# Places for loaded weights, the split of y, and how the last heads' rows are turned, in a two-layer decoder trunk

## The chip, the cores and the metric

The kernel runs on one core of one Trainium2 chip. The metric is the device time of one execution in microseconds (us). The core has five engines with queues of their own: TensorE (PE; its weight loads are listed as PEld), VectorE (DVE), ScalarE (ACT), GpSimd (POOL) and SyncE (SP). Here SP's queue issues every DMA, in order. An engine that waits at an instruction runs nothing that is queued behind it.

## The reference

Two pre-norm residual layers and a final norm, over 1024 positions of width 1024, all in float32:

```python
x = x + lru_mixer(rms_norm(x, g0), ...)   # layer 0: conv, gates, linear recurrence, width 1536
x = x + fox_mixer(rms_norm(x, g1), ...)   # layer 1: attention, 16 heads of 64
return rms_norm(x, final_g)

def fox_mixer(h, w_in, b_f, w_out):
    u = h @ w_in                            # q, k, v, gate: 1024 each; 16 forget logits
    cum = cumsum(log_sigmoid(f_logit + b_f))
    logits = (q @ k.T) / 8 + (cum[query] - cum[key])      # causal
    o = softmax(logits) @ v
    return (o * silu(gate)) @ w_out
```

## The kernel before

Every large product is done in three passes: a float32 operand is split into a high part in float32r (`to_hi`) and a low rest (`to_lo`), and TensorE adds high·high, low·high and high·low. So weights, values, probabilities and the gated outputs y all pass through a pair of splitting instructions: `to_hi` mostly on ACT, `to_lo` on DVE or POOL.

**Loaded weights.** A DMA brings weights into a place of the tag `wf` of the pool `wpool`, and the split writes them to places of `wh` and `wl` (four of each). A place is free again once its last reader is done. `wf` has three places. The largest user sets a place's size: the first values' weights, two blocks of 256 values and 16 forget logits, 2304 bytes in each partition; all others need 2048 or less. `wf` is used for layer 0's weights (`weights`, `out_weights`, `split_gates`), for q, k and gate weights and most of the output weights (`weights`), for the values of heads 4 to 15 (`value_weights`, in three groups of four heads) and for the last two pairs' output weights (`late`).

**Attention.** `values(0)` makes the values of heads 0 to 3 and the forget logits; `forget` turns the logits into cumulative sums. Then head after head, each in two passes, written out by hand as strings: `"1.0.1.10.1..0"` for a head's first pass, `"10.1.0.10.1.0.0"` for its second (`LAST` has longer ones for heads 12 to 15, with more dots). In the first pass 0 is a step of `weigh(hd, 0)` (queries 0 to 511 times values) and 1 a step of `maxima(hd, 1)` (scores, maximum and exponential of query rows 7, 6, 5, 4, a row being 128 queries). In the second pass 0 is `weigh(hd, 1)` and 1 is `maxima(hd + 1, 0)` (rows 3 to 0). A dot is a piece of `fill`, some six matmuls of the projections of the next pair of heads (for heads 12 to 15: of the output projection, `partial` and `turned`), and one step of `side`.

Each row's scores S lie in one of two places of PSUM (tag `S`); DVE masks and finds the maximum (L773), ACT makes the exponential p (L778).

**Turning p.** Values are multiplied with p turned, keys on partitions. `by_dma(hd, c)` says which way: by TensorE (`transpose`, L61, into a PSUM place of tag `S`, then split from there by ACT and DVE), or for part of the blocks "far": for the last two of a half's four rows, DVE turns 32 by 32 blocks (L733), a DMA writes them to DRAM (`turnd`, L738 and L740), and four DMAs read them back (`pp<-turnd`, L745), whereupon ACT and DVE split them. Before, only head 0's first half is turned by TensorE alone.

**y.** `side` of a second pass is `settle(hd)`: it fetches the reciprocals of the sums (`recb`), has POOL scale the gate with them (L813) and, for an odd head, multiply the pair's first half of y by it (`gated`, L911), and then `put_away(hd, 0)`: ACT splits y (`yh`), DVE makes the rest in place (`yo`), two DMAs store both to DRAM (`y1d`, L928). The second half's `put_away(hd, 1)` stands in `put_later`, the side of the next head's first pass, at its fourth dot. This holds for pairs 0 to 5; `load_y` fetches them back during head 13. `yo` has two places, so that a pair's first half of y takes the place of the pair before's.

**Order.** The program is written in this order, but a planner reorders each engine's queue by its own estimate of when operands are ready; `issue_after` ties an instruction behind another one of its engine (`seen`: the last exponential on ACT; `masked`: the last maximum on DVE).

**Memory.** Layer 1's pools `tu` and `at` lie where layer 0's `x`, `y`, output weights and squares lay; in `at` the tags lie in the order of their first use, in before: `yo`, `recb`, `sg`, `ph`, `p4`, `p5`, `pp1`, `turn`, and so on.

Of the kernel before, what the change touches and what calls it, by code (L numbers as in the profile page):

```python
# [17 lines left out]
P = 128  # L18
SEQ = 1024
HALF = 512  # L20
KT = 8
# [17 lines left out]
def trunk(ctx: ExitStack, tc: tile.TileContext, xt, w0, wg, wo0, pc, gn, gf, w1, wv, wf, bf, wo1, out):  # L39
# [60 lines left out]
    def split_weights(src, shape, hi_eng, lo_eng, parts=wpool):  # L100
        n = shape[0] * shape[1]
        room = -(-n // 64) * 64
        a = wpool.tile([P, room], F32, tag="wf", name="wf", bufs=3)[:, :n]
        b = parts.tile([P, room], F32R, tag="wh", name="wh")[:, :n]
        c = parts.tile([P, room], F32R, tag="wl", name="wl")[:, :n]
        wt, hi, lo = (t.rearrange("p (a b) -> p a b", a=shape[0]) for t in (a, b, c))
        for part, sl in src:
            nc.sync.dma_start(wt[:, :, sl], part)
        to_hi(b, a, hi_eng)
        to_lo(c, a, b, lo_eng)  # L110
        return [(hi[:, k], lo[:, k]) for k in range(shape[0])]
# [67 lines left out]
    with ExitStack() as l0:  # L179
# [85 lines left out]
        gate_weights = {}  # L265

        def split_gates(n):
            wt = wpool.tile([P, 4, P], F32, tag="wf", name="wgf", bufs=3)[:, :2]
            nc.sync.dma_start(wt, wg[n])
            wgh = tmp.tile([P, 2, P], F32R, tag="wgh", name="wgh", bufs=2)  # L270
            wgl = tmp.tile([P, 2, P], F32R, tag="wgl", name="wgl", bufs=2)
            to_hi(wgh, wt, nc.vector)
            to_lo(wgl, wt, wgh, nc.vector)
            gate_weights[n] = wgh, wgl
# [80 lines left out]

        def out_weights(g, d0, parts=wpool):

            wt = wpool.tile([P, 4, P], F32, tag="wf", name="wf", bufs=3)
            for j in range(2):
                nc.sync.dma_start(wt[:, 2 * j : 2 * j + 2], wo0[d0 + j, :, 2 * g : 2 * g + 2])  # L360
            hi = parts.tile([P, 4, P], F32R, tag="wh", name="wh")
            lo = parts.tile([P, 4, P], F32R, tag="wl", name="wl")
            to_hi(hi, wt, nc.scalar)
            to_lo(lo, wt, hi, nc.vector)
            return [[(hi[:, 2 * j + i], lo[:, 2 * j + i]) for i in range(2)] for j in range(2)]
# [136 lines left out]
    with ExitStack() as l1:  # L502
# [24 lines left out]
        def value_weights(g, parts):  # L527

            waiting = []
            for k in range(0, KT + 2, 2):  # L530
                if k < KT:
                    wt = wpool.tile([P, 2, 256], F32, tag="wf", name="wf", bufs=3)
                    nc.sync.dma_start(wt, wv[g, :, k : k + 2])
                    waiting.append(wt)
                if k:
                    own = wpool if k <= 4 else vwpool
                    hi = own.tile([P, 2, 256], F32R, tag="wh", name="wh")
                    lo = own.tile([P, 2, 256], F32R, tag="wl", name="wl")
                    with tc.issue_after(seen[0].ins):
                        to_hi(hi, waiting[0], nc.scalar)  # L540
                    with tc.issue_after(masked[0].ins):
                        to_lo(lo, waiting.pop(0), hi, nc.vector)
                    parts += [(hi[:, i], lo[:, i]) for i in range(2)]
                yield

        def values(g, parts):

            ex = 0 if g else HEADS
            for k in range(0, 0 if g else KT, 2):
                src = [(wv[g, :, k : k + 2], slice(0, 256)), (wf[:, k : k + 2], slice(256, 256 + ex))]  # L550
                parts += split_weights(src, (2, 256 + ex), nc.scalar, nc.gpsimd)
                if k == 2:
                    yield
            Vs[2 * g], Vs[2 * g + 1] = [], []
            for st in range(8):
                if ex and st % 2:
                    pt = ps.tile([P, SEQ], F32, tag="S", name="vps")[:, : 256 + ex]
                else:
                    pt = ps.tile([P, 256 + ex], F32, tag="g", name="vps")
                c = (st % 4) * P  # L560
                for k in range(KT):
                    xh, xl = hT[st // 4][k]
                    wh, wl = parts[k]
                    xh, xl = xh[:, c : c + P], xl[:, c : c + P]
                    matmul(pt, xh, wh, start=k == 0, stop=False)
                    matmul(pt, xl, wh, start=False, stop=False)
                    matmul(pt, xh, wl, start=False, stop=k == KT - 1)
                    if k % 4 == 1:
                        yield
                r_ = rms1[st // 4][:, st % 4 : st % 4 + 1]  # L570
                for a in range(2):
                    v = vpool.tile([P, 4, HD], F32R, tag=f"v{st}", name=f"v{st}", bufs=2)
                    src = pt[:, a * P : (a + 1) * P].rearrange("p (b d) -> p b d", b=2)
                    to_hi(v[:, 0::3], src, nc.scalar, scale=r_)
                    nc.vector.scalar_tensor_tensor(v[:, 1:3], src, r_, f32(v[:, 0::3]), ALU.mult, ALU.subtract)
                    Vs[2 * g + a].append(v)
                if ex:
                    nc.vector.tensor_scalar(fz[:, st], pt[:, 256:], r_, None, ALU.mult)
# [71 lines left out]
        def forget(half):  # L650
            cs = slice(half * HALF, (half + 1) * HALF)
            pt = ps.tile([P, HALF], F32, tag="O", name="fps")
            for i in range(4):
                if half and i > 1:
                    yield
                with tc.issue_after(pe[0].ins):
                    transpose(pt[:HEADS, i * P : (i + 1) * P], fz[:, half * 4 + i], ident)
            e_ = at.tile([HEADS, HALF], F32, tag="ph", name="e", bufs=3)
            parts = [at.tile([HEADS, HALF], F32R, tag=t, name="cp", bufs=1) for t in (("p4", "p5"), ("pp1", "turn"))[half]]
            hi, lo = parts  # L660
            nc.scalar.activation(e_, pt[:HEADS], AF.Softplus, bias=bft, scale=-1.0)
            nc.vector.tensor_tensor_scan(
                cum[:, cs], unit, e_, cum[:, HALF - 1 : HALF] if half else 0.0, ALU.mult, ALU.subtract
            )
            to_hi(hi, cum[:, cs], nc.vector)
            to_lo(lo, cum[:, cs], hi, nc.vector)
            for i in range(2):
                nc.sync.dma_start(cumd[:, i, cs], f32(parts[i]))
            for hd in range(2):
                if half == 0:  # L670
                    load(hd, cs, (0,) if hd == 0 else ())
# [47 lines left out]
            return two_rows[c][:, r * size : r * size + n]  # L719

        def by_dma(hd, c):
            return hd > 0 or c == 1

        written, turns = [None], {}

# [89 lines left out]
        def weigh(hd, c, sub=slice(0, HALF)):  # L815
# [6 lines left out]
            O = ps.tile([P, HALF], F32, tag="O", name="O")[:, : sub.stop - sub.start]  # L822
            b = 4 * c

            def cover(r):
                first = [max(j, r) for j in range(r + 2)]
                return [(j, (q - b) * P, (r + 2 - q) * P) for j, q in enumerate(first)]

            def packed(pieces):
                units = []  # L830
# [3 lines left out]
                    units[-1].append(piece)  # L834
                return units

            mine = cover(b) if sub.start == 0 else []
            away = cover(b + 2) if sub.stop == HALF else []
            n = len(away) - 1 if by_dma(hd, c) else 0
            mine, away = packed(mine + away[n:]), packed(away[:n])  # L840
            steps = [(z[i : i + 2], z is away) for z in (mine, away) for i in range(0, len(z), 2)]
            count = [0, 2 * sum(map(len, mine + away))]

# [86 lines left out]
        def settle(hd):  # L930
            yield
            yield
            with tc.issue_after(written[0].ins):
                fetch_sums(hd)
            yield
            scale(hd)
            gated(hd, 0)
            yield
            put_away(hd, 0)

        def put_later(hd):
            yield
            yield
            yield
            put_away(hd, 1)

        def beside(*gens):
            for _ in itertools.zip_longest(*gens):
# [136 lines left out]
        def late():  # L1085

            for half in range(2):
                wh, wl = (kqpool.tile([P, 8, P], F32R, tag=f"qk{p}{half}", name=f"wo{p}") for p in "hl")
                for b in range(2):
                    wt = wpool.tile([P, 4, P], F32, tag="wf", name="wf", bufs=3)  # L1090
                    for d in range(2):
                        nc.sync.dma_start(wt[:, 2 * d : 2 * d + 2], wo1[half * 4 + b * 2 + d, :, 6:8])
                    sl = slice(4 * b, 4 * b + 4)

                    with tc.issue_after(seen[0].ins):
                        to_hi(wh[:, sl], wt, nc.scalar)
                    to_lo(wl[:, sl], wt, wh[:, sl], nc.vector)
                    yield
                late_w.append((wh, wl))
# [148 lines left out]
```

## Time and profile before

| | |
|---|---|
| median of 3 runs | 1134.2 us (1132.59 to 1134.7) |
| the profiled execution | 1137.31 us, span 1135.5 us from first to last instruction |
| PE busy | 1097.4 us (97%) |
| DVE, ACT, POOL busy | 797.6 (70%), 581.6 (51%), 171.8 us (15%) |
| mean granted TensorE clock | 0.981 |
| DMA | 152.89 MB, mean 135 GB/s |

The profiled execution is 3.1 us above the median; sums over its rows are sums against 1137.31. A time in a row is in us from the span's start. In a timeline row the first number is the start, the second the time taken (of all instructions of the row), x3 the count, and a bracket gives the engine's idle time just before and what ended it. Layer 0 runs until about 451 us, the attention from about 486 us to 1100 us. A head takes two passes of together about 30 us; head 1's second pass ends at about 565 us.

### The profile page before, as it was taken

What the parts mean: (1) busy time and instruction counts of PE and PEld (TensorE: products, weight loads), DVE (VectorE), ACT (ScalarE), POOL (GpSimd) and SP (SyncE); (2) the same over time, 40 slices, a digit from 0 to 9 for tenths busy, and PEclk for the clock granted to TensorE, in tenths of its full rate; (3) what the DMA queues carried; (4) which work ended last, traced back from release to release, by engine and by line L of the source; (5) the groups of instructions that cost most, each with busy time, mean ns of one, the idle gap of its engine ahead of it and who ended that gap; (6) DMA issues with size and microseconds to landing.
All of it is one profiled execution on the core that took longest, in us unless ns stands there. A gap on an engine that the chain in (4) does not pass through costs nothing.

```text
span 1135.5 us, 15920 instructions
## 1 busy us (share of the span) xinstructions
PE 1097.4 (97%) x5627; PEld 928.5 (82%) x5627; DVE 797.6 (70%) x1291; ACT 581.6 (51%) x1038; POOL 171.8 (15%) x120
## 2 busy tenths in 40 slices
PE   9999999999999999999999999899998999988998
PEld 7787888888888888978788988788887898867776
DVE  8898765677566897667787487874777847647545
ACT  8587344445445656445555355554555534424335
POOL 2312212212111102311111011101111010110010
PEclk9999999999999999999999999999998999989899
DMA  5111111111112124355767267672676735897554
GB/s 217 59 61 41 53 42 52 47 51 53 41 52 66 45 81 145 93 162 151 217 175 201 78 179 200 194 194 84 176 199 181 197 94 169 311 259 225 177 177 185
DMA packets 107511, 152.89 MB, mean 135 GB/s; under 512 B 27844, under 2 KB 59204, under 8 KB 107432
## 3 DMA queue, kind: packets, MB, share of 16 engines
q1 hardware_dynamic: 107432, 151.88, 45.1%
q8 instruction: 44, 0.72, 0.3%
q14 instruction: 35, 0.29, 0.1%
HBM read 87.02 MB, written 39.65 MB: 112 GB/s over the span
## 4 chain that ended last, share of the span: by engine, by line
PE 78%; DMA 7%; DVE 5%; issue 4%; ACT 3%; POOL 1%; SPq 1%; ACTq 0%; DVEq 0%; POOLq 0%
PE gps L57 28%; PE ops L57 16%; PE ups L57 10%; PE vps L57 8%; PE S L57 5%; PE O L57 5%; PE turn L57 3%; PE gate L57 2%; PE pt L61 2%; DMA wf<-in_w 1%; DVE pl L98 1%; DMA recd<-rc 1%; DMA recb<-recd 1%; DMA yhl<-y1d 1%; ACT pp L778 1%
## 5 line engine op out<-in xcount | busy, mean ns | idle before, releaser
L57 PE MATMUL gps<-hh,wh 128*128 128x512 f32 x576 | 231.0, 401 | 0.0
L57 PE MATMUL gps<-hh,wl 128*128 128x512 f32 x576 | 227.0, 394 | 0.1
L57 PE MATMUL gps<-hl,wh 128*128 128x512 f32 x576 | 226.4, 393 | 0.0
L87 ACT CAST wh<-wf 128x512 fp32r<-128x512 f32 (+2 forms) x156 | 94.1, 607 | 131.7 <-PE ops L57 42.7
L98 POOL TENSOR_TENSOR wl<-wf,wh 128x512 fp32r<-128x512 f32 (+1 forms) x60 | 99.3, 1659 | 378.7 <-ACT wh L87 261.9
L57 PEld LDWEIGHTS gps<-hl,wh 128*128 128x128 f32 x576 | 109.1, 189 | 23.8
L57 PEld LDWEIGHTS gps<-hh,wl 128*128 128x128 f32 x576 | 109.6, 190 | 18.7 <-POOL wl L98 0.6
L57 PEld LDWEIGHTS gps<-hh,wh 128*128 128x128 f32 x576 | 109.6, 190 | 18.5
L813 POOL TENSOR_TENSOR sg<-sg,recb 64x512 f32<-64x512 f32 x32 | 44.7, 1414 | 494.7 <-DMA recb<-recd 494.7
L773 DVE CUSTOM_DVE_ANT_0 S<-S,mask 128x512 f32<-128x512 f32 (+7 forms) x128 | 97.3, 760 | 27.3 <-PE S L57 26.4
L57 PE MATMUL S<-T,U 128*128 128x512 f32 (+7 forms) x384 | 94.9, 357 | 10.7 <-ACT pp L778 10.7
L778 ACT ACTIVATE pp<-S,m 128x512 f32<-128x512 f32 (+1 forms) x64 | 54.3, 849 | 90.3 <-DVE m L773 90.3
L57 PEld LDWEIGHTS S<-T,U 128*128 128x128 f32 (+1 forms) x384 | 69.4, 195 | 26.5 <-ACT pp L778 13.5
L57 PE MATMUL O<-ph,v 128*128 128x256 f32 x320 | 82.3, 286 | 2.6 <-ACT ph L87 2.6
L98 DVE TENSOR_TENSOR wl<-wf,wh 128x512 fp32r<-128x512 f32 x96 | 66.3, 697 | 25.6 <-ACT wh L87 25.4
L98 DVE TENSOR_TENSOR pl<-pp,ph 128x512 fp32r<-128x512 f32 x94 | 64.5, 718 | 27.7 <-ACT ph L87 24.4
L375 DVE TENSOR_TENSOR x<-x,ops 128x512 f32<-128x512 f32 x80 | 54.2, 682 | 41.4 <-PE ops L57 41.4
L57 PE MATMUL O<-pl,v 128*128 128x256 f32 x320 | 81.0, 290 | 0.4 <-DVE pl L98 0.3
L57 PE MATMUL vps<-wh,hh 128*128 128x256 f32 (+1 forms) x256 | 74.6, 292 | 3.2 <-DVE sg L699 1.4
L57 PE MATMUL ups<-hh,wl 128*128 128x512 f32 x192 | 75.1, 391 | 0.8 <-POOL wl L98 0.8
L57 PE MATMUL ups<-hh,wh 128*128 128x512 f32 x192 | 75.7, 395 | 0.1
L57 PE MATMUL ups<-hl,wh 128*128 128x512 f32 x192 | 75.2, 392 | 0.2 <-DVE hl L232 0.2
(170 smaller groups left out, 2398.7 us busy)
## 6 DMA issues: line engine op xcount, KB each, us to landing
wf<-in_w SPq DMA_DIRECT2D x100, 256.0 KB
turnd<-turn SPq DMA_DIRECT2D x32, 448.0 KB
pp<-turnd SPq DMA_DIRECT2D x64, 224.0 KB
wf<-in_wo SPq DMA_DIRECT2D x64, 128.0 KB
U<-qkh SPq DMA_DIRECT2D x64, 128.0 KB
T<-qkh SPq DMA_DIRECT2D x28, 256.0 KB
turnd<-turn SPq DMA_DIRECT2D x15, 384.0 KB
pp<-turnd SPq DMA_DIRECT2D x60, 96.0 KB
```

Source lines behind the costliest of these rows:

```text
L57: pe[0] = nc.tensor.matmul(*args, **kw)
L61: pe[0] = nc.tensor.transpose(*args)
L87: nc.scalar.copy(hi, src)
L98: return eng.tensor_tensor(lo, src, f32(hi), ALU.subtract)
L375: nc.vector.tensor_tensor(x, x, pt, ALU.add)
L773: masked[0] = nc.vector.tensor_tensor_reduce(S[:, :n], S[:, :n], mask[:, SEQ - n :], -1.0, -NEG, ALU.add, ALU.min, accum_out=m)
L778: seen[0] = nc.scalar.activation(p, S[:, :n], AF.Exp, bias=m, scale=-1.0, accum_out=sums[:, i : i + 1])
L813: nc.gpsimd.tensor_tensor(sg, sg, recs[hd // 2][rows, part], ALU.mult)
```

## The change

1. `wf` has four places (the pool's default), each of 2048 bytes. The first values' weights no longer go through places of 2304 bytes: `values(0)` loads the 256 values' columns into `wf`, and the 16 logits' columns of all eight blocks by one DMA into `own` (tag `rc`). The split parts lie in places of `at` that the attention uses later: `p4`, `p5`, `pp0`, `turn`, three in `pp1`, one in `sg`. Each pair of blocks takes two `to_hi` and two `to_lo` (columns of values, columns of logits) in place of one and one.
2. `forget` keeps its sums' parts in `xp`, `xp` (first half) and `pp1`, `p5` (second half).
3. `put_away(hd, 0)` moves from `settle` (second pass of an odd head, fifth dot) to `put_later` (first pass of the next head, third dot); `put_away(hd, 1)` moves from the fourth dot of that pass to the fifth.
4. `by_dma` holds for 0 < 2·hd + c < 27: head 13's second half and heads 14 and 15 are turned by TensorE alone. In halves turned so, a block of keys is turned and multiplied for all four query rows at once, not for two and two.

```diff
-        a = wpool.tile([P, room], F32, tag="wf", name="wf", bufs=3)[:, :n]
+        a = wpool.tile([P, room], F32, tag="wf", name="wf")[:, :n]
...
         def values(g, parts):
             ex = 0 if g else HEADS
+            if g == 0:
+                own = at.tile([P, KT, ex], F32, tag="rc", name="own", bufs=1)
+                nc.sync.dma_start(own, wf)
+                size = 2 * (256 + ex)
+                big = at.tile([P, 3, 576], F32R, tag="pp1", name="wh0", bufs=1)
+                room = [at.tile([P, 576], F32R, tag=t, name="wh0", bufs=1) for t in ("p4", "p5", "pp0", "turn")]
+                room += [big[:, i] for i in range(3)]
+                room.append(at.tile([P, 576], F32R, tag="sg", name="wh0"))
             for k in range(0, 0 if g else KT, 2):
-                src = [(wv[g, :, k : k + 2], slice(0, 256)), (wf[:, k : k + 2], slice(256, 256 + ex))]
-                parts += split_weights(src, (2, 256 + ex), nc.scalar, nc.gpsimd)
+                wt = wpool.tile([P, 2, 256], F32, tag="wf", name="wf")
+                nc.sync.dma_start(wt, wv[g, :, k : k + 2])
+                hi, lo = (z[:, :size].rearrange("p (a b) -> p a b", a=2) for z in room[k : k + 2])
+                for src, cs in ((wt, slice(0, 256)), (own[:, k : k + 2], slice(256, 256 + ex))):
+                    to_hi(hi[:, :, cs], src, nc.scalar)
+                    to_lo(lo[:, :, cs], src, hi[:, :, cs], nc.gpsimd)
+                parts += [(hi[:, i], lo[:, i]) for i in range(2)]
...
-            ... for t in (("p4", "p5"), ("pp1", "turn"))[half]]
+            ... for t in (("xp", "xp"), ("pp1", "p5"))[half]]
...
         def by_dma(hd, c):
-            return hd > 0 or c == 1
+            return 0 < 2 * hd + c < 27
...
-            def cover(r):
-                first = [max(j, r) for j in range(r + 2)]
-                return [(j, (q - b) * P, (r + 2 - q) * P) for j, q in enumerate(first)]
+            def cover(r0, r1):
+                first = [max(j, r0) for j in range(r1)]
+                return [(j, (q - b) * P, (r1 - q) * P) for j, q in enumerate(first)]
...
-            mine = cover(b) if sub.start == 0 else []
-            away = cover(b + 2) if sub.stop == HALF else []
-            n = len(away) - 1 if by_dma(hd, c) else 0
-            mine, away = packed(mine + away[n:]), packed(away[:n])
+            if by_dma(hd, c):
+                away = cover(b + 2, b + 4)
+                mine = packed(cover(b, b + 2) + away[-1:])
+                away = packed(away[:-1])
+            else:
+                mine, away = packed(cover(b + sub.start // P, b + sub.stop // P)), []
...
         def settle(hd):
...
             scale(hd)
             gated(hd, 0)
-            yield
-            put_away(hd, 0)
 
         def put_later(hd):
-            yield
-            yield
-            yield
-            put_away(hd, 1)
+            for c in range(2):
+                yield
+                yield
+                put_away(hd, c)
```

More of the change, by code (lines that the diff above doesn't have):

```diff
@@ L267, in split_gates @@
         def split_gates(n):
-            wt = wpool.tile([P, 4, P], F32, tag="wf", name="wgf", bufs=3)[:, :2]
+            wt = wpool.tile([P, 4, P], F32, tag="wf", name="wgf")[:, :2]
             nc.sync.dma_start(wt, wg[n])
@@ L356, in out_weights @@
         def out_weights(g, d0, parts=wpool):
-            wt = wpool.tile([P, 4, P], F32, tag="wf", name="wf", bufs=3)
+            wt = wpool.tile([P, 4, P], F32, tag="wf", name="wf")
             for j in range(2):
@@ L531, in value_weights @@
                 if k < KT:
-                    wt = wpool.tile([P, 2, 256], F32, tag="wf", name="wf", bufs=3)
+                    wt = wpool.tile([P, 2, 256], F32, tag="wf", name="wf")
                     nc.sync.dma_start(wt, wv[g, :, k : k + 2])
@@ L548, in values @@
             ex = 0 if g else HEADS
-            for k in range(0, 0 if g else KT, 2):
-                src = [(wv[g, :, k : k + 2], slice(0, 256)), (wf[:, k : k + 2], slice(256, 256 + ex))]
-                parts += split_weights(src, (2, 256 + ex), nc.scalar, nc.gpsimd)
+            if g == 0:
[6 more added lines that the diff above has]
+                room.append(at.tile([P, 576], F32R, tag="sg", name="wh0"))
+            for k in range(0, 0 if g else KT, 2):
+                wt = wpool.tile([P, 2, 256], F32, tag="wf", name="wf")
+                nc.sync.dma_start(wt, wv[g, :, k : k + 2])
[4 more added lines that the diff above has]
+                parts += [(hi[:, i], lo[:, i]) for i in range(2)]
                 if k == 2:
@@ L658, in forget @@
             e_ = at.tile([HEADS, HALF], F32, tag="ph", name="e", bufs=3)
-            parts = [at.tile([HEADS, HALF], F32R, tag=t, name="cp", bufs=1) for t in (("p4", "p5"), ("pp1", "turn"))[half]]
+            parts = [at.tile([HEADS, HALF], F32R, tag=t, name="cp", bufs=2 if t == "xp" else 1) for t in (("xp", "xp"), ("pp1", "p5"))[half]]
             hi, lo = parts
@@ L1089, in late @@
                 for b in range(2):
-                    wt = wpool.tile([P, 4, P], F32, tag="wf", name="wf", bufs=3)
+                    wt = wpool.tile([P, 4, P], F32, tag="wf", name="wf")
                     for d in range(2):
```

## The prediction

> **What bounds the kernel now.** I read the page's first part, then who waited for whom on TensorE, then its busy time in stretches of 25 us, and then the timeline around each stretch that falls short.
>
> ```profile
> span 1135.5 us, 15920 instructions
> PE 1097.4 (97%) x5627; PEld 928.5 (82%) x5627; DVE 797.6 (70%) x1291; ACT 581.6 (51%) x1038; POOL 171.8 (15%) x120
> ```
>
> TensorE is the bound: every other engine has a quarter of the span to spare. So the time can fall only by TensorE's waits and by what a slower clock costs, and it rises by each matmul added. The waits:
>
> ```profile
> PE S L57 <- ACT pp L778: 10.7, 4, 3.7
> PE ops L57 <- ACT wh L87: 5.4, 1, 5.4
> PE O L57 <- ACT ph L87: 2.6, 1, 2.6
> PE turn L57 <- DVE xp L1009: 2.4, 1, 2.4
> PE ops L57 <- DVE xp L1009: 1.9, 1, 1.9
> PE vps L57 <- DVE wl L98: 1.9, 2, 0.9
> PE vps L57 <- ACT wh L87: 1.2, 2, 1.0
> ```
>
> Columns: total us, times, longest. Now the stretches; the last three columns are the granted clock, the DMA share and GB/s:
>
> ```profile
> core 0: us, PE busy (x) PEld busy (x) DVE busy (x) ACT busy (x) POOL busy (x), PEclk, DMA share, GB/s
> 50.00:75.00 25.00, 25.00 (x112) 20.70 (x111) 20.78 (x20) 20.04 (x23) 4.63 (x3) 1.00 0.11 37
> 550.00:575.00 25.00, 21.64 (x110) 17.99 (x109) 16.41 (x31) 11.03 (x23) 5.54 (x4) 0.93 0.66 188
> 625.00:650.00 25.00, 24.27 (x182) 23.83 (x183) 10.51 (x24) 8.33 (x22) 1.29 (x1) 0.93 0.23 73
> 700.00:725.00 25.00, 21.30 (x110) 18.05 (x108) 17.78 (x34) 12.41 (x26) 5.62 (x4) 0.93 0.53 168
> 750.00:775.00 25.00, 22.95 (x136) 19.88 (x135) 17.41 (x34) 12.42 (x28) 4.13 (x3) 0.93 0.88 224
> 850.00:875.00 25.00, 21.75 (x104) 18.02 (x102) 18.34 (x35) 13.73 (x28) 3.71 (x3) 0.86 0.56 168
> 1000.00:1025.00 25.00, 20.22 (x84) 16.40 (x83) 10.97 (x19) 8.00 (x17) 5.35 (x4) 0.80 0.84 240
> 1050.00:1075.00 25.00, 23.32 (x104) 19.31 (x105) 13.49 (x27) 8.94 (x19) 3.13 (x3) 0.86 0.52 177
> ```
>
> Layer 0 (50 to 75 us as its pattern) is full, so a fourth place of `wf` has nothing to gain there. The short stretches are of three kinds. **A**: the ends of heads 1, 5 and 9 (565, 709, 853 us). **B**: the values of the next four heads (624, 767 us, little at 912 us). **C**: heads 13 to 15 (1000 to 1100 us). Each wait costs twice: after it the clock is below 1. A mean of 0.93 over 25 us is 1.75 us of full-speed work lost, 0.86 is 3.5, 0.80 is 5.0.
>
> **The change part by part.**
>
> *Split of y one pass later.* Around the end of head 1:
>
> ```profile
> 560.12 2.53 POOL L813 TENSOR_TENSOR sg<-sg,recb 64x512 f32<-64x512 f32 x2 [28.44 <-DMA recb<-recd]
> 562.72 1.28 POOL L911 TENSOR_TENSOR yo<-yo,sg 128x512 f32<-128x512 f32 x1
> 564.04 0.62 ACT L87 CAST yh<-yo 128x512 fp32r<-128x512 f32 x1 [4.97 <-POOL yo L911]
> 564.69 0.69 DVE L98 TENSOR_TENSOR yo<-yo,yh 128x512 fp32r<-128x512 f32 x1 [3.65 <-ACT yh L87]
> ```
>
> `recb` lands, POOL scales, POOL multiplies; ACT stands 4.97 us at `yh`, DVE behind it at `yo`, and the maximum and exponential of the next S row queue behind both. TensorE runs out of S places: that is three of the four waits on `pp` (10.7 us, at most 3.7 each; I count 10.2). With the clock, 1.75 + 1.75 + 3.5 = 7.0, A costs 17.2 us. One pass later POOL has long finished, and the same six `yh`, six `yo` and twelve DMAs are issued as before. What comes late next is the place of y itself. In the pass that they move into:
>
> ```profile
> 571.48 1.01 ACT L778 ACTIVATE pp<-S,m 128x896 f32<-128x896 f32 x1 [2.51 <-DVE m L773]
> 575.33 0.32 SPq L738 DMA_DIRECT2D turnd<-turn  x1
> 577.89 2.60 SPq L745 DMA_DIRECT2D pp<-turnd  x4
> 579.46 0.58 ACT L901 COPY yo<-O 64x512 f32<-64x512 f32 x1 [0.31 <-PE O L57]
> 580.53 0.60 SPq L928 DMA_DIRECT2D y1d<-yo  x1
> 1093.46 4.26 DMA x1d<-xp
> ```
>
> The third dot follows row 6, whose exponential ends at 572.5. So ACT splits to 573.2, DVE makes the rest by 574 to 575.5 (a maximum and a 1.1 us transposition compete), and SP stores at about 576, ahead of the `pp<-turnd` issues at 577.9, which wait for row 6 in DRAM. ACT's copy at 579.5 overwrites the place that this store reads: new in after, where the store stands in the same pass as the copy. A store of this size took 4.26 us at 1093 us (the last row, from the chain that ended last); uncrowded it may be less. So ACT waits 0 to 1 us at six passes: I take +1 in all, bound +5. I credit A with -15.5, bounds -17.2 and 0. Moving the second half's split one dot later costs nothing: its place is wanted a whole pass later.
>
> *Heads turned by TensorE.* Blocks turned go from 12 to 26 for the second halves of heads 13 to 15 and from 4 to 10 for the first halves of 14 and 15: 3·14 + 2·6 = 54 more. The prices:
>
> ```profile
> L61 PE MATMUL pt<-ident,p 128*128 128x128 f32 x224 | 32.7, 274 | 0.3
> 954.80 0.49 PE L61 MATMUL pt<-ident,p 128*128 128x128 f32 x3
> L733 DVE STREAM_TRANSPOSE turn<-pp 128x896 f32<-128x896 f32 x32 | 35.5, 1109 | 14.3 <-ACT pp L778 13.2 <-DMA turnd<-turn 0.9
> ```
>
> Three in a row take 0.49 us, one 0.274: (0.49 - 0.274)/2 = 0.108 us apart. 54·0.108 = +5.8 us; busy time over count, 32.7/224 = 0.146, gives +7.9 as the upper bound. I take 5.8, as they come in runs. Fewer, wider products save a little over the same columns: 0, bound -1. DVE loses six transpositions of 1.1 us and four shorter ones; it isn't the bound, so nothing. Splits stay as many, read from PSUM. Two more S places are used in each second half; fill covers them (bound +3). SP loses 28 issues, with 6·448 + 12·224 + 2·384 + 8·96 KB. What waited for them:
>
> ```profile
> 990.76 0.33 SPq L738 DMA_DIRECT2D turnd<-turn  x1
> 1001.34 2.61 SPq L745 DMA_DIRECT2D pp<-turnd  x4
> 1046.24 0.52 SPq L108 DMA_DIRECT2D wf<-in_wo  x1
> ```
>
> Head 13's last row is written only at 990.8, behind the loads of y, and read back from 1001.3; TensorE waits 2.6 us for its split, then 1.9 us for a sum whose load stood behind the read-back, and the clock loses 5.0: 9.5 us. Turned by TensorE this chain is gone, though the 6 MB of y still pass: -8.5, bounds -9.5 and -3.
>
> *The fourth place.* At 1046 us TensorE waits 5.4 us for `wh`, whose load is issued at 1046.24; `late` holds places of `wf` until its splits, which are tied behind the exponentials. With the clock (3.5): 8.9 us. One more place lets the load go earlier by about one split, some 3 us, and SP no longer stands at `pp<-turnd`: -5, bounds -8.9 and 0. For B:
>
> ```profile
> 616.42 0.54 SPq L533 DMA_DIRECT2D wf<-in_wv  x1
> 621.66 0.62 ACT L87 CAST wh<-wf 128x512 fp32r<-128x512 f32 x1 [3.59 <-DMA wf<-in_w]
> 613.63 1.29 DVE L98 TENSOR_TENSOR wl<-wf,wh 128x512 fp32r<-128x512 f32 x2
> 622.31 2.69 DVE L98 TENSOR_TENSOR wl<-wf,wh 128x512 fp32r<-128x512 f32 x2 [3.08 <-ACT wh L87]
> 622.84 1.60 POOL L911 TENSOR_TENSOR yo<-yo,sg 128x512 f32<-128x512 f32 x1
> ```
>
> The group's last weights are loaded only at 616.4, and ACT stands 3.6 us for loads. B's waits are 1.9 + 1.2 and some behind other DVE work, about 4.5 us, and the clock's 1.75 twice: 8 us. With the place and without the `yh` in this stretch: -5, bounds -8 and 0.
>
> The Trainium skill bears on that term ("SBUF — State Buffer", SBUF: two separate sides): VectorE and GpSimd share a pair of ports under an exclusive lock, and the loser blocks for the whole instruction. The trace agrees: two `wl` took 1.29 us alone and 2.69 us beside POOL's 1.60 us. POOL's work stays there, so by the rule alone about 1.4 us of each group's wait would stay.
>
> *First values.* POOL and ACT run eight splits for four, SP five loads for eight. The parts now lie in `at` by order of first use, where layer 0's last two y lay, and `own` in one of those places; y is read until the last product of layer 0 at 451 us. So `own` and most parts start 2 to 6 us later than in before, where the first split ran at 444 us. TensorE has the second half of q and k to run meanwhile, whose weights now find free places. I take +1.5, bounds 0 and +6: the nearest rows, the waits for `wl` and `wh`, were about 1 us each.
>
> **Sum.** +1 - 15.5 + 5.8 - 8.5 - 5 - 5 + 1.5 = -25.7 us against the profiled execution's 1137.3, so 1111.6; it stood 3.1 us above the median of 1134.2, so 1108.5, say **1108 us**.
>
> **The rivals.**
>
> *R1, slower: y's place.* If the planner puts the y store behind the `pp<-turnd` issues, as it did for the second half (580.53, above), it lands at 580.5 + 4.3 = 584.8, and ACT stands 5.3 us at the copy, as it stood 4.97 in A. A's price, (10.2 + 7.0)/3 = 5.7 us, would then be paid at six heads: +34 in place of +1, 1141. For it: the row at 580.53. Against: that split came a row later than the new one will. It decides from 27/6 = 4.5 us a head.
>
> *R2: the end doesn't gain.* The loads of y and the output weights queue on SP whoever turns p; then the 8.5 and 5 don't come, and TensorE pays the 5.8: 1122. For it: the DMA share of 0.84 at 1000 us and the wait of 5.4 us for a weight, not for p. Against: head 13's wait names `ph`.
>
> *R3: turning slows the clock.* Each half turned by TensorE holds up to 26 instructions that load and stream 128 columns only; if these don't keep the clock up, the five halves lose up to one slow stretch of 1.75 us each, 8.8 us: 1117. Against: layer 1's stretches hold such turns throughout, and only those with waits fall below 1. The Trainium skill says this ("TensorE: Matmul & The Clock Gate", Part 4: PE-mode transpose): transposes don't count as busy for the clock gate, and one takes about 275 ns in a kernel. By its figure 54 would cost an estimated 14.9 us; the rows show 274 ns for one alone but 108 ns apart.
>
> *R4: the change adds little.* A's other queue, `recb` and POOL, is untouched and the splits still run: A might reappear at the next instruction that needs y, and B with it. Then C alone works: 1108 + 20.5 = 1128.
>
> **How the numbers follow.** My case 0.62, R2 0.15, R3 0.05, R4 0.05, R1 0.13. The predicted time is my case's, 1108; its own range, by the bounds of A to C, is 1094 to 1119. To leave out no more than two in ten, the range goes to R4: 1094 to 1130. A measurement here tells about 0.2%, 2.3 us. R1 gives slower 0.10, same 0.02, faster 0.01; the others are faster: faster 0.88, same 0.02, slower 0.10.
>
> **What would show it.** TensorE's wait for `pp` falls from 10.7 us to under 2, with clock 1.00 at the ends of heads 1, 5 and 9, and `yh` no longer waits for POOL; a copy `yo<-O` waiting for a DMA at heads 2, 4, 6 would be R1. `pt` counts 316; the stretch from 1000 us loses its wait for `ph`. The wait of `ops` for `wh` halves; if it stays at 5, the place was not its cause. A gap ahead of the first `vps` near 451 us above 3 us would show the first values dearer than I took. Wrong would also be a planner's new order that opens waits where there are none now; none of my terms covers that.

## The result and the profile after

| | before | after |
|---|---|---|
| median | 1134.0 us (4 runs) | 1125.7 us (4 runs, 1125.0 to 1126.9) |
| ratio | | 0.9930, 95% interval 0.9912 to 0.9947 |
| profiled execution | 1137.3 us, span 1135.5 | 1125.4 us, span 1123.6 |
| mean granted clock | 0.981 | 0.991 |

The kernel became faster by 8.3 us; 26 were forecast. The profiled execution of after stands 0.3 us under its median, that of before 3 us over its own, so the two traces differ by 11.9 us of span. A ratio is formed over the executions and is not that of the two medians; a gain given right behind a ratio below is worked out from it. The page's first part and TensorE's waits of after (total us, times, longest):

```profile
span 1123.6 us, 15882 instructions
PE 1090.8 (97%) x5645; PEld 923.7 (82%) x5645; DVE 794.6 (71%) x1280; ACT 580.4 (52%) x1041; POOL 168.2 (15%) x124
```

```profile
PE sscol L57 <- DVE sq L166: 6.0, 1, 6.0
PE S L57 <- ACT pp L791: 3.9, 8, 1.0
PE rsrow L57 <- DVE rs L153: 2.5, 1, 2.5
PE vps L57 <- DVE wl L98: 2.4, 2, 1.4
PE ops L57 <- ACT wh L87: 1.9, 1, 1.9
PE ops L57 <- DVE wl L98: 1.8, 1, 1.8
```

The two longest stops, `sscol` and `rsrow`, are new. The waits that before showed have shrunk: S for `pp` is at most 1.0 us at a time (3.7 before), `O` for `ph` is gone, `ops` for the split output weights is 1.9 + 1.8 (5.4 before). Stretches of after:

```profile
core 0: us, PE busy (x) PEld busy (x) DVE busy (x) ACT busy (x) POOL busy (x), PEclk, DMA share, GB/s
450.00:475.00 25.00, 16.47 (x92) 14.68 (x90) 12.76 (x26) 10.98 (x24) 15.17 (x17) 0.73 0.52 157
550.00:575.00 25.00, 25.00 (x141) 21.43 (x140) 20.78 (x42) 14.14 (x32) 3.38 (x3) 1.00 0.78 210
625.00:650.00 25.00, 24.01 (x179) 22.60 (x178) 12.38 (x26) 9.73 (x24) 5.45 (x4) 1.00 0.41 125
1000.00:1025.00 25.00, 23.69 (x117) 19.72 (x116) 14.46 (x27) 9.35 (x21) 5.16 (x4) 1.00 0.62 203
1025.00:1050.00 25.00, 21.26 (x102) 17.38 (x102) 15.04 (x31) 9.87 (x22) 2.93 (x2) 0.93 0.47 150
```

and the same stretch behind layer 0 in before, which the prediction had no reason to show, since it was full:

```profile
450.00:475.00 25.00, 24.75 (x190) 23.56 (x189) 19.21 (x43) 11.34 (x23) 8.14 (x8) 1.00 0.42 117
```

So the seven stretches that fell short in before all stand at clock 1.00. What is left of the wait for the output weights now falls into 1025 to 1050 us (0.93), and a hole that was not there before takes half of the gain back: 92 matmuls against 190 in the same 25 us, at clock 0.73. The start of row 7's exponential in each head dates the gains and losses. Heads 0, 12 and 14, from ACT's timeline, first before, then after:

```profile
505.76 1.12 ACT L778 ACTIVATE pp<-S,m 128x1024 f32<-128x1024 f32 x1 [0.79 <-DVE m L773]
...
939.06 1.12 ACT L778 ACTIVATE pp<-S,m 128x1024 f32<-128x1024 f32 x1 [1.18 <-DVE m L773]
...
1023.11 1.12 ACT L778 ACTIVATE pp<-S,m 128x1024 f32<-128x1024 f32 x1 [2.19 <-DVE m L773]
```

```profile
517.89 1.12 ACT L791 ACTIVATE pp<-S,m 128x1024 f32<-128x1024 f32 x1 [1.42 <-DVE m L786]
...
935.80 1.12 ACT L791 ACTIVATE pp<-S,m 128x1024 f32<-128x1024 f32 x1 [1.17 <-DVE m L786]
...
1013.12 1.12 ACT L791 ACTIVATE pp<-S,m 128x1024 f32<-128x1024 f32 x1 [2.13 <-DVE m L786]
```

After minus before: +12.1 us at head 0, -3.3 at head 12, -10.0 at head 14, -11.9 at the end of the span. Three parts, then: the first values +12.1, heads 0 to 12 -15.4, the rest -8.6.

**The hole.** The timeline of after behind layer 0:

```profile
456.72 3.55 PE L57 MATMUL sscol<-onesf,sq 128*128 128x1 f32 x16 [6.02 <-DVE sq L166]
460.64 0.51 SPq L551 DMA_DIRECT2D own<-in_wf  x1
460.67 2.18 ACT L87 CAST wh<-wf 128x512 fp32r<-128x512 f32 x4
462.78 2.08 PE L57 MATMUL rsrow<-rs,onesf 128*128 128x512 f32 x2 [2.51 <-DVE rs L153]
463.87 1.22 PE L57 MATMUL vps<-wh,hh 128*128 128x272 f32 x1
```

and of before:

```profile
448.18 0.65 ACT L87 CAST wh<-wf 128x544 fp32r<-128x544 f32 x1 [0.57 <-PE ops L57]
451.56 0.36 PE L57 MATMUL vps<-wh,hh 128*128 128x272 f32 x1 [0.25 <-DVE x L484]
459.40 1.84 PE L57 MATMUL sscol<-onesf,sq 128*128 128x1 f32 x16
```

`sscol` sums the squares of the second half of x; it must wait for layer 0's last sum, square and addition on DVE. In before TensorE fills that wait with the values of the first half of the positions (`vps` from 451.56, `sscol` only at 459.40 and with no idle time ahead of it). In after the load of `own` is issued, and the splitting of the first values' weights begins, only 0.4 us after `sscol` has ended (456.72 + 3.55 = 460.27), not after y's last product at about 451. So the work that covered the wait for `sscol` now comes behind `sscol`.

### The profile page after: what moved, and what is told of

The parts are those of the page before. It is cut to its first block, busy times and chain, and to the rows that moved or that the text cites. A ratio compares the mean times of both kernels' runs of the same rounds, so it can differ in the third digit from the quotient of the medians.

```text
span 1123.6 us, 15882 instructions
## 1 busy us (share of the span) xinstructions
PE 1090.8 (97%) x5645; PEld 923.7 (82%) x5645; DVE 794.6 (71%) x1280; ACT 580.4 (52%) x1041; POOL 168.2 (15%) x124
## 4 chain that ended last, share of the span: by engine, by line
PE 43%; DVE 6%; DMA 5%; ACT 2%; issue 2%; SPq 0%; POOL 0%; ACTq 0%; DVEq 0%; POOLq 0%
PE gps L57 16%; PE vps L57 8%; PE S L57 5%; PE O L57 4%; PE ops L57 4%; PE turn L57 2%; PE pt L61 2%; DVE pl L98 2%; DMA yhl<-y1d 1%; DVE S L786 1%; ACT pp L791 1%; DMA wf<-in_w 1%; ACT ph L87 1%; DVE wl L98 1%; DMA T<-qkh 1%
## 5 line engine op out<-in xcount | busy, mean ns | idle before, releaser
L87 ACT CAST wh<-wf 128x512 fp32r<-128x512 f32 (+1 forms) x156 | 93.8, 607 | 135.0 <-PE gps L57 43.7
L98 POOL TENSOR_TENSOR wl<-wf,wh 128x512 fp32r<-128x512 f32 x56 | 88.9, 1594 | 387.2 <-ACT wh L87 340.6
L98 DVE TENSOR_TENSOR wl<-wf,wh 128x512 fp32r<-128x512 f32 x96 | 69.4, 729 | 22.2 <-ACT wh L87 20.5
L57 PE MATMUL vps<-wh,hh 128*128 128x256 f32 (+1 forms) x320 | 81.5, 293 | 0.2
L57 PE MATMUL O<-pl,v 128*128 128x256 f32 (+3 forms) x302 | 77.1, 290 | 2.6 <-DVE pl L98 2.3
L57 PE MATMUL O<-ph,v 128*128 128x256 f32 (+3 forms) x302 | 78.5, 288 | 0.0
L57 PE MATMUL ops<-yh,wh 128*128 128x512 f32 x192 | 75.2, 392 | 0.0
```

The lines of the kernel that those rows point to most:

```text
L57: pe[0] = nc.tensor.matmul(*args, **kw)
L87: nc.scalar.copy(hi, src)
L98: return eng.tensor_tensor(lo, src, f32(hi), ALU.subtract)
```

## The experiments

**Each half of the change by itself.** The theory after the first look: the later split and the turning gain what they were made for, and the first values' places alone bring the hole. The rival: the parts act on each other, and the shortfall is in the attention.

Before with part 3 alone:

```diff
             gated(hd, 0)
-            yield
-            put_away(hd, 0)
 ...
-            yield
-            yield
-            yield
-            put_away(hd, 1)
+            for c in range(2):
+                yield
+                yield
+                put_away(hd, c)
```

> The kernel before with part 3 alone (both halves of y split in the next head's first pass). Theory: this part took the waits at the ends of heads 1, 5 and 9 with their slow clock (17.2 us by the rows of before); about 1134 - 15 = 1119 us, the stretches at 550, 700 and 850 us at clock 1.00. Rival: in the whole change it was the other parts that took them, or y's place makes new waits at heads 2 to 12: then 1130 us or more.

Measured: 1124.9 us against 1136.7, ratio 0.9892 (0.9870 to 0.9914), so -12.3 us. Its waits and two of its stretches:

```profile
PE S L57 <- ACT pp L778: 4.1, 9, 0.8
PE vps L57 <- ACT wh L87: 2.4, 3, 1.2
PE vps L57 <- DVE wl L98: 1.3, 2, 0.7
```

```profile
625.00:650.00 25.00, 24.69 (x184) 23.52 (x184) 10.94 (x25) 8.37 (x21) 1.28 (x1) 1.00 0.12 38
750.00:775.00 25.00, 22.90 (x161) 20.91 (x160) 13.16 (x27) 10.20 (x25) 5.60 (x4) 1.00 0.54 143
```

A's long waits are gone, and C's remain (`O` for `ph` 3.5 us, `ops` for `wh` 3.7), as they should. B's stretches (0.93 before) have clock 1.00 too, with three places of loaded weights. But B's waits themselves (`vps` for `wl` and `wh`) are no shorter: 3.7 us, 3.1 before. What went is the slow clock behind them.

Before with part 4 alone:

```diff
-            return hd > 0 or c == 1
+            return 0 < 2 * hd + c < 27
 ...  # weigh's pieces for halves without far rows, as in the change
```

> The kernel before with part 4 alone (head 13's second half and heads 14 and 15 turned by TensorE). Theory: heads 13 to 15 and the end became 8.6 us shorter in the whole change; if turning alone did it, about 1126 us, and the wait of 5.4 us for an output weight near 1046 us is gone too. Rival: that wait went by the fourth place; then turning alone gives 9.5 - 5.8 = about 4 us, 1130 us, and the wait for a weight stays.

Measured: 1128.1 us against 1136.7, ratio 0.9923 (0.9900 to 0.9945), so -8.7 us. Two waits and the stretch at 1000 us (before: busy 20.22, clock 0.80):

```profile
PE S L57 <- ACT pp L778: 9.9, 5, 3.3
PE ops L57 <- ACT wh L87: 3.2, 1, 3.2
```

```profile
1000.00:1025.00 25.00, 25.00 (x128) 21.24 (x127) 14.08 (x27) 10.53 (x23) 5.13 (x4) 1.00 0.64 197
```

A stays (9.9 us for `pp`), and the waits for `ph` and for the sum behind it are gone. The theory had the wait for the output weights gone as well; 3.2 us for `wh` and 1.1 for `wl` stay (5.4 for `wh` before).

Before with parts 1 and 2 alone (the change with parts 3 and 4 undone):

> The kernel before with parts 1 and 2 alone (four places of 2048 bytes, the first values' parts in layer 1's pool). Theory: TensorE stands for 8 to 9 us after layer 0 and at half clock for 13 us, about +12 us, and the fourth place takes some 5 us of the waits before the values of heads 4 to 15: about 1141 us. Rival: the hole after layer 0 needs the other parts' changed order to open; then no hole, and 1128 us.

Measured: 1144.9 us against 1136.7, ratio 1.0067 (1.0045 to 1.0089): slower by 7.6 us. It has the hole of after, with the same 6.0 and 2.5 us of waiting:

```profile
450.00:475.00 25.00, 16.47 (x88) 14.66 (x87) 12.65 (x26) 10.69 (x23) 15.14 (x17) 0.73 0.54 158
625.00:650.00 25.00, 23.25 (x157) 21.75 (x156) 15.39 (x30) 11.59 (x27) 5.42 (x4) 0.93 0.65 180
775.00:800.00 25.00, 22.52 (x152) 20.87 (x151) 12.51 (x22) 9.05 (x22) 5.41 (x4) 0.93 0.47 143
```

Without turning, the fourth place does cut the wait for the output weights (`wh` 0.5 and `wl` 1.0 us), which gives some of the hole back. The values of heads 4 to 15, where 5 us were expected, gain nothing from it: `vps` waits 3.5 us for `wl` and 0.5 for `wh` (3.1 together before), and B's two slow stretches are still there.

Before with parts 3 and 4, without 1 and 2:

> Parts 3 and 4 without parts 1 and 2: three places of 2304 bytes, the first values' weights as before. Theory: the hole after layer 0 is the price of parts 1 and 2, so without them the kernel is faster than the whole change by 12 us less what the fourth place gives (3 to 5): about 1117 us. Rival: the fourth place carried the gains of heads 13 to 15, then 1124 us or more.

Measured: 1116.3 us against 1136.7, ratio 0.9818 (0.9793 to 0.9842), -20.7 us: the sum of the two alone, 12.3 + 8.7 = 21.0. They don't hinder each other, and this version is faster than both kernels.

**What the first values wait for.** T1: a tile of layer 1's pool `at` waits for everything of layer 0's released pools, squares included. Rivals: the four places of loaded weights or the doubled splits make the hole; or only one of the two things moved into `at` does.

The change with the parts and `own` kept out of `at`:

```diff
-                own = at.tile([P, KT, ex], F32, tag="rc", name="own", bufs=1)
+                own = vwpool.tile([P, KT, ex], F32, tag="own", name="own", bufs=1)
-                big, room = ...             # eight tiles of at
+                # k < 4:  hi, lo = vwpool.tile([P, 544], F32R, tag="wh" / "wl"), two blocks each
+                # k >= 4: hi, lo = wpool.tile([P, HALF], F32R, tag="wh" / "wl"), one block each
```

> The changed kernel with its four places, its later split and its turning, but the first values' parts and forget weights kept out of layer 1's pool: blocks 0 to 3 in the value pool on the right side, blocks 4 to 7 one to a place of the weight pool, the forget weights in the value pool. Theory T1: a tile of layer 1's pool waits for everything of layer 0's released pools, the last squares and stores among it, so the splits cannot start before 460 us. Then the hole of 6.0 + 2.5 us and the 13.65 us of half clock behind layer 0 go, the values' matmuls stand ahead of sscol again, head 0's row-7 exponential starts within 1.5 us of the kernel before, and the ratio to before is 0.980 (0.977 to 0.983), 2 us under later split plus turning alone. Rival T2: the hole comes from how the four places of loaded weights turn over, or from splitting each piece in two: then head 0 stays 8 to 12 us late, ratio 0.990 or more.

Measured: 1113.9 us against 1137.6, ratio 0.9786 (0.9756 to 0.9815), the fastest version of all. The hole is gone, and head 0's row 7 starts at 506.01, 0.25 us later than in before:

```profile
450.00:475.00 25.00, 25.00 (x192) 23.82 (x191) 18.18 (x43) 11.15 (x25) 6.95 (x10) 1.00 0.35 97
750.00:775.00 25.00, 23.40 (x158) 21.80 (x157) 14.30 (x27) 10.37 (x25) 5.89 (x4) 0.93 0.51 144
```

Still four places, still two pieces for each block: the rival T2 falls. The second row shows that one of B's slow stretches is back, with the later split and four places both in. The same with three places:

> The run above with three places of 2048 bytes for loaded weights in place of four; nothing else differs. By the prediction's terms the fourth place was worth 5 us at the weights awaited near 1046 us and 5 us at the splits of the values of later heads: 10 us over the run above, ratio 0.989. By what the first four runs showed (later split plus turning without the fourth place 0.982; the places alone 6.5 us at 1046 us, a wait that the turning shortens too): 2 us over the run above, ratio 0.982.

Measured: 1116.2 us, ratio 0.9815 (0.9784 to 0.9846), 2.3 us more than with four on the same chip (3.3 by the ratios); the intervals overlap, but a worth of 10 us is out. B's slow stretch at 750 us is there with three as with four. The clearest difference between the two traces is at the output weights. TensorE's wait for them, then the stretch around it, first with four places:

```profile
PE ops L57 <- ACT wh L87: 2.4, 1, 2.4
```

```profile
1020.00:1045.00 25.00, 22.17 (x111) 17.98 (x111) 16.02 (x33) 10.35 (x24) 2.96 (x2) 1.00 0.48 149
```

and with three, where the second wait, for `wl`, grows from 0.4 to 1.3 us and the clock is 0.86:

```profile
PE ops L57 <- ACT wh L87: 3.1, 1, 3.1
```

```profile
1020.00:1045.00 25.00, 20.60 (x90) 16.71 (x89) 12.93 (x26) 7.91 (x19) 2.93 (x2) 0.86 0.43 137
```

Only `own` put back into `at` (the edit below), then only the parts (the eight tiles of `at` as in the change, `own` in `vwpool`):

```diff
-                own = vwpool.tile([P, KT, ex], F32, tag="own", name="own", bufs=1)
+                own = at.tile([P, KT, ex], F32, tag="rc", name="own", bufs=1)
```

> The first of these runs with only the forget weights (own, 512 bytes a partition) put back into layer 1's pool. T1: their load is issued when the last of layer 0's pool is released, near 460 us, and every block needs 16 columns of them, so the hole comes back almost whole: head 0 8 to 12 us late, ratio 0.988 to 0.992. Rival T3: the places of the parts themselves make the hole, not the load: no hole, ratio as the first run.

> The changed kernel with only the forget weights taken out of layer 1's pool (into the value pool, so loaded early); the parts stay in it. T1: the splits still wait for the pool, but not for a load behind it: the hole is shorter by the load's 2.5 us at most, head 0 7 to 12 us late, ratio 0.988 to 0.993. Rival T4: the load was all of it: no hole, ratio 0.980.

Measured: 1124.4 us, ratio 0.9884 (0.9857 to 0.9911), and 1124.2 us, ratio 0.9883 (0.9854 to 0.9913). Either of them alone brings nearly the whole hole, 10.5 and 10.3 us over the version that keeps both out of `at`. TensorE has the same wait in both, 6.57 us ahead of `sscol` with `own` in `at` and 6.02 with the parts there. T3 and T4 fall: each thing is enough by itself.

What the two wait for is harder to read from their own starts. With `own` in `at`, `sscol` ends at 461.57 and the load is issued at 461.91, but right behind another issue of SP that ends at 461.80; with the parts in `at`, `sscol` ends at 461.48 and the first split starts at 461.89, but right behind ACT's `rms<-sscol`. A place in the queue would give such starts too. A cleaner witness is `unit`, a tile of `at` (tag `recb`) that every version has: POOL fills it with ones, and it reads nothing. In after, then with the parts and `own` kept out (with `sscol`'s row), with `own` in, with the parts in:

```profile
460.33 0.52 POOL L660 MEMSET unit<- 16x512 f32 x1 [0.79 <-PE sscol L57]
...
460.56 1.84 PE L57 MATMUL sscol<-onesf,sq 128*128 128x1 f32 x16
462.46 0.52 POOL L665 MEMSET unit<- 16x512 f32 x1 [0.84 <-PE sscol L57]
...
461.63 0.51 POOL L665 MEMSET unit<- 16x512 f32 x1 [0.20 <-PE sscol L57]
...
461.55 0.51 POOL L660 MEMSET unit<- 16x512 f32 x1 [0.79 <-PE sscol L57]
```

POOL stands idle and starts 0.06 to 0.07 us after `sscol`'s end (460.27, 462.40, 461.57, 461.48), wherever that falls, and without the hole as well. So a tile of `at` waits for the last reading of layer 0's squares, as T1 says. The tiles of the other pool, `tu`, don't: in after `mask` and `U` are filled from 457.46 and 456.74 on, before `sscol` has ended. Whether a tile of `at` waits for all that this pool covers, or for what lies beneath the tile itself, no run tells apart for certain. By the sizes in the kernel and the order of the tags `tu` would cover x alone, and `unit` would lie where y lay, not over the squares, which speaks for the first; but no run shows the addresses.

**What a turned block costs.** The version that keeps the parts and `own` out of `at`, with all halves from head 11 on turned by TensorE:

```diff
-            return 0 < 2 * hd + c < 27
+            return 0 < 2 * hd + c < 22
```

> The first kernel of the last four (parts kept out of layer 1's pool, four places) with more halves turned by TensorE: all from head 11 on, in place of all from the second half of head 13 on. That adds 2 second halves of 14 blocks and 3 first halves of 6, 46 blocks, where no wait for a row read back was seen. If a turned block costs its distance of 0.108 us and nothing else, +5.0 us, ratio to before 0.983. If a block costs what one alone takes in the trace, 0.274 us, +12.6 us, ratio 0.990. If the turning costs TensorE nothing that shows, because the chains through DRAM that go hold it up elsewhere, no change, 0.979.

Measured: 1116.0 us against 1135.9, ratio 0.9812 (0.9777 to 0.9847), 0.0026 above that version: 3 us, and from -2 to +8 by the intervals. That excludes 12.6 us and decides nothing between 0 and 5.0.

## Why the prediction was wrong in size

The direction was right, and the size failed at one term. By its own steps:

| step | predicted | measured | by |
|---|---|---|---|
| first values | +1.5, bounds 0 and +6 | +12.1 | head 0 in the traces; +10.5 and +10.3 for either thing alone |
| split of y later, with y's place | -15.5 + 1 | -12.3, with B in it | part 3 alone |
| turning, with head 13's read-back | +5.8 - 8.5 | -8.7 | part 4 alone |
| fourth place, at the end and for B | -5 - 5 | -2.3 | four places against three |

The measured column adds up to -11.2 us: near the traces' -11.9, and 2.9 us beyond the medians' -8.3 (whose interval is -10.0 to -6.0). This rest isn't settled.

**First values: the step that failed.** "y is read until the last product of layer 0 at 451 us. So `own` and most parts start 2 to 6 us later." The address was thought to decide, and y the only thing in the way. The runs show the release at the end of `sscol`, 460.3, 9 us later. The second half of the error was the cover: "TensorE has the second half of q and k to run meanwhile". In the program's order that half stands behind the values, and the trace has its first product at 491.0 (479.0 in before), when the values are done; so nothing was left to run. Whether it could have been put ahead is not tested. And the price of a stop of 8.5 us (6.0 + 2.5) is not 8.5: from 454.5 to 468.0 the clock was 0.50, and the 8.8 us that TensorE worked in that time cost 4.4 more (`sscol` itself took 3.55 us in place of 1.84). By this estimate 12.9, measured 12.1. The term of +1.5 was sized by waits of about 1 us elsewhere, and its bound of +6 by a start 2 to 6 us later; neither holds a wait for the squares. The text did name the sign to look for, a gap above 3 us near 451, and it came.

**Split of y.** Right in mechanism: with part 3 alone 4.1 of the 10.7 us of waits for `pp` stay, in nine pieces of at most 0.8 us. In after the copy `yo<-O` waited for the store of y once, for 0.8 us, and the store stood ahead of the read-back, so R1 did not come:

```profile
584.15 0.32 SPq L943 DMA_DIRECT2D y1d<-yo  x1
585.89 2.58 SPq L758 DMA_DIRECT2D pp<-turnd  x4
```

`yh` no longer waits for POOL. The gain of 12.3 us includes B's clock, which the prediction credited apart: A and B together were 20.5 there, of which 15.4 came in after.

**Values of heads 4 to 15.** The place did not do what it was credited with: alone it left both slow stretches and 4.0 us of waits for `wl` and `wh`. The later split alone took both stretches to clock 1.00 and left 3.7 us of waits. Nor is it a sure cure: with both in and the hole gone, 2.0 us of waits were left and one slow stretch was back (750 us, 0.93). Why the split took the slow clock away is thus not shown; of the 5 us credited, at most the 3.4 us of two slow spells came by it. The Trainium skill's rule weighed there ("SBUF — State Buffer", SBUF: two separate sides: VectorE and GpSimd lock each other out of a shared pair of ports) is borne out in after as well: two `wl` took 2.66 us beside a POOL instruction of 1.61 us, where two alone took 1.29 in before.

```profile
631.32 2.66 DVE L98 TENSOR_TENSOR wl<-wf,wh 128x512 fp32r<-128x512 f32 x2 [2.95 <-ACT wh L87]
631.82 1.61 POOL L926 TENSOR_TENSOR yo<-yo,sg 128x512 f32<-128x512 f32 x1
```

**Turning.** The group's busy time rose by more than was priced; blocks of `p` and `pp` in after:

```profile
L61 PE MATMUL pt<-ident,p 128*128 128x128 f32 x224 | 34.5, 274 | 0.0
L61 PE MATMUL pt<-ident,pp 128*128 128x128 f32 x92 | 18.3, 274 | 1.2 <-ACT pp L791 1.2
```

The count is 316, as forecast. With 32.7 + 9.7 before (the second for 38 blocks of `pp`) that is 10.4 us for 54 blocks, 0.193 each, not 0.108. Yet part 4 alone gained 8.7, where the terms gave 2.7: what went with the chain through DRAM was worth more than the 8.5 credited. The waits for `ph` (2.6) and for the sum (1.9) are gone in that run, and its mean clock is 0.989 against 0.981, by estimate some 9 us of full speed over the span where 5.0 were credited. R2 thus fell. R3 fell too: clock 1.00 from 1000 to 1025 us with the turns in it. The rule cited for it (the Trainium skill, "TensorE: Matmul & The Clock Gate", Part 4: PE-mode transpose), that the full clock doesn't engage for transposes, does not show where they stand among other matmuls; its 275 ns is the mean of one here, 274, but 46 more blocks did not cost 46 times that.

**Fourth place.** The wait for the output weights near 1046 us was credited to the place alone, though the term itself says "SP no longer stands at `pp<-turnd`", which is the turning's doing. For `wh` and `wl` together TensorE waits 5.4 us in before, 4.3 with turning alone and 1.5 with the places alone; with turning and the later split, 4.4 with three places and 2.8 with four. So once the rows are turned, the place saves some 2 to 3 us of the 10 credited.

R4 fell with part 3's -12.3. Without the hole the rest of the sum comes out near: -27.2 us by its terms, -23.7 measured (1113.9 against 1137.6) in the version that keeps the first values out of `at`. A part of that is luck: turning gave 6.0 us more than its terms, the fourth place 7.7 less.

## What to carry to other kernels

Before a buffer is moved into the memory of an earlier stage, ask for the last reader of anything that this stage releases, not only for the last reader at the address, and ask what TensorE runs in the time until then: if it is the very work that the buffer feeds, the wait has lost its cover. A small late piece is enough, as 512 bytes of logits' weights cost as much as all eight tiles. Where two remedies act on one wait, price the second one with the first in place.

## What the runs showed of the hardware

The clock's price comes in steps. Behind the wait of `turn` in before it is 0.50 for the 3 us shown first, with 0.84 and 0.75 in the half microseconds on either side: 0.16 + 3.0 + 0.25 = 3.4 us at half speed. In the hole of after it is 0.50 for four times as long (second row; 0.89 and 0.95 on either side, 13.7 us in all):

```profile
1098.50:1101.50 3.00, 3.00 (x10) 2.51 (x11) 0.55 (x2) 0.31 (x2) 0.00 (x0) 0.50 0.40 149
454.50:468.00 13.50, 8.77 (x32) 7.44 (x33) 7.07 (x15) 4.61 (x13) 10.98 (x14) 0.50 0.59 162
```

Over 25 us most short stretches show 0.93, 0.86, 0.80 or 0.73, which are one, two, three and four such spells (1 - 3.4/50 = 0.93). Whether a wait of 2.4 us costs one isn't fixed: that of `turn` in before (2.45 us) did, that for the output weights with four places and the parts kept out of `at` (2.43 us; 1.00, above) did not.

The busy time listed for turned blocks overstates their cost: in the run with 46 more it rose from 34.3 + 18.2 us to 36.1 + 26.0, by 9.6 us, and the time by about 3, with the interval given there. A part of the price may be hidden in that 3: the run without the 46 has one slow spell at 750 us (0.93, 1.7 us) in its trace, the one with them has none.
